# Windowed attention heads: two query blocks share one 512-column product per key tile

## The chip, the core and the metric

The kernel runs on one core of one Trainium2 chip. The metric is the device time of one execution in microseconds (us). Three runs of the kernel before gave 1479.55, 1479.58 and 1482.57 us; the median, 1479.58 us, is what a changed kernel is compared with.

## What is computed

The reference is a two-layer encoder trunk over 1024 tokens of width 1024. Only one part of its first layer matters here: eight "B" heads of width 64 in grouped-query attention (four query heads to one of two key heads), where a query sees the keys within 128 positions, plus a learned sink in the softmax:

```python
def window_gqa(q, k, v, sink, rel_bias):      # BLOCK = WINDOW = 128
    ...
    def one(args):                            # one block of 128 queries
        i, qblk = args
        kb = lax.dynamic_slice_in_dim(kp, i * BLOCK, 384, axis=1)
        vb = lax.dynamic_slice_in_dim(vp, i * BLOCK, 384, axis=1)
        s = jnp.einsum('bqkgd,bskd->bkgqs', qblk, kb) * scale + bias
        s = jnp.where(valid, s, -jnp.inf)
        m = jnp.maximum(jnp.max(s, axis=-1, keepdims=True), sk)
        p = jnp.exp(s - m)
        denom = jnp.sum(p, axis=-1, keepdims=True) + jnp.exp(sk - m)
        return jnp.einsum('bkgqs,bskd->bqkgd', p / denom, vb)
```

So each block of 128 queries meets its own tile of 128 keys and the tile on either side (two tiles in all at the two ends of the sequence).

## The kernel before, in words

All values are float32. A product is made from two rounded halves of each operand (a high part `h` and the remainder `l`, both in the format fp32r), so that one product becomes two or three matrix multiplications.

The program is built in Python; a planner then lays out the instructions of each engine from estimated times, priorities and dependencies. Program order sets the priority. `ahead(kind)` moves a step forward by a number of places (in this phase: scores 20, exponentials 60, splitting of a bank 150, closing 120; transposes and value products 0). `issue_after(x)` puts what follows behind instruction `x` on the same engine.

The phase "l0" works through layer 0: A heads and memory heads first, then the **band stage**, four calls of `window_pair` (L685) from `even`, each for two B heads (`i` = 0, 1 below, the "pair"). The stage lies about between 515 and 667 us of the span; the output projection of layer 0 (`out_project`, L1341 to L1376 in the profile) follows, and its first pieces are mixed into the last pair.

A call of `window_pair` goes over four groups `g` of two query blocks (`b` = 0, 1), that is blocks 2g and 2g+1:

- **Scores** (L710, L711): for each block and head, two multiplications into a bank `sa`; VectorE adds the bias, takes the running minimum and writes the tile `P` (L714). `P` holds both heads of one block; there are six such buffers, which later also receive the residual `xT` of the output projection (L1373).
- **Softmax**: ScalarE's exponentials (L725), VectorE's reciprocal (L727), then four **normalisations** on GpSimd (L732), in the order block 0 head 0, block 0 head 1, block 1 head 0, block 1 head 1.
- **Values**: `todo` lists the pairs (block, key tile), block 0 first: six pairs, or five in the first and last group. They are taken two at a time, in two or three steps `t`. In a step TensorE **transposes** four tiles of 128x128 of `P` (two pairs, two heads; L133) into one PSUM bank `tr` (two such banks); the transposes of steps 0 and 1 are written together ahead of step 0. ScalarE then copies the bank to `ph` (L125) and VectorE makes `pl` (L549). For each pair of the step two **value products** (L757) follow, one with the 256 columns of `ph` and one with those of `pl`, into the bank `pv` (one only). The columns of a pair go to two separate runs of 128 in that bank, since the bank is ordered head, block, query.
- **Closing**: the lower half of the bank is copied to `bt`, and L767 adds the halves into `y`.

Between these steps `pull(pulls)` inserts pieces of a projection that had been put off (L242: three multiplications of 512 columns each piece; two pieces at a time, one in the third pair). Such pieces stand behind the last score or transpose written before them. They are what TensorE does while the other engines prepare `P`, `ph` and `pl`.

Of the kernel before, what the change touches and what calls it, by code (L numbers as in the profile page):

```python
# [47 lines left out]
            c=(("P", "P"), ("P", "P"), ("P", "P"), ("yb", "yb"))),  # L48
       dict(y=(("P", "P", "q", "q", "v"), ("k", "k", "k", "k", "q", "q"), ("H",) * 6, ("H",) * 6, ("P", "P", "q", "q", "v"),
               ("k", "k", "k", "k", "q", "q"), ("H",) * 6),  # L50
            c=(("H", "H"), ("H", "H"), ("mk", "sg"), ("yb", "yb"))))
# [13 lines left out]
class Trunk:  # L65
# [619 lines left out]
    def window_pair(self, qs, ks, v, kv, h0, sink, y, pulls, side, lead=0):  # L685

        nc = self.nc
        kh, kl = ks
        bias = self.st("bias", [128, 2, 384])
        nc.sync.dma_start(bias, self.io["band"][h0:h0 + 2].rearrange("h p k -> p h k"))  # L690
        for g in range(4):
            st = self.tiny()
            nm, sm, r = (st[:, 4 * j:4 * j + 4] for j in range(3))
            pts = []
            o = self.ps("pv")
            ov = o.rearrange("p (h b q) -> p h b q", h=2, b=2)
            spans = []
            for b in range(2):
                blk = 2 * g + b
                lo, hi = max(0, blk - 1), min(8, blk + 2)  # L700
                n = (hi - lo) * 128
                bo = (lo - blk + 1) * 128
                spans.append((lo, hi, n))
                s = self.ps("sa", (128, 2, 512))
                pt = self.st("P", [128, 2, 385])
                nc.scalar.activation(pt[:, :, n:n + 1], sink[:, h0:h0 + 2][:, :, None], AF.Copy)
                for i in range(2):
                    q = qs[i][:, blk * 128:(blk + 1) * 128]
                    with self.ahead("score"):
                        nc.tensor.matmul(s[:, i, :n], q, kh[:, lo * 128:hi * 128], start=True, stop=False)  # L710
                        self.fence = nc.tensor.matmul(s[:, i, :n], q, kl[:, lo * 128:hi * 128], start=False, stop=True)  # L711
                    with self.ahead("exp"):
                        j = 2 * b + i
                        nc.vector.tensor_tensor_reduce(pt[:, i, :n], s[:, i, :n], bias[:, i, bo:bo + n], op0=OP.add,  # L714
                                                       op1=OP.min, scale=-1.0, scalar=sink[:, h0 + i:h0 + i + 1],
                                                       accum_out=nm[:, j:j + 1])
                pts.append(pt)
                if lead and g == 0:
                    self.pull(lead)
            with self.ahead("exp"):  # L720
                for b in range(2):
                    n = spans[b][2]
                    for i in range(2):
                        j = 2 * b + i
                        nc.scalar.activation(pts[b][:, i, :n + 1], pts[b][:, i, :n + 1], AF.Exp, bias=nm[:, j:j + 1],  # L725
                                             scale=-1.0, accum_out=sm[:, j:j + 1])
                nc.vector.reciprocal(r, sm)  # L727
                for b in range(2):
                    n = spans[b][2]
                    for i in range(2):  # L730
                        j = 2 * b + i
                        normal = nc.gpsimd.tensor_scalar(pts[b][:, i, :n], pts[b][:, i, :n], r[:, j:j + 1], 0.5,  # L732
                                                         op0=OP.mult, op1=OP.mult)
                self.normal = normal
            if g < 2:
                with self.tc.issue_after(normal.ins):
                    next(side, None)
            todo = [(b, c) for b in range(2) for c in range(spans[b][0], spans[b][1])]
            self.pull(pulls)
            made = {}  # L740
            for t in range(0, len(todo), 2):
                self.later_job(normal)
                two = todo[t:t + 2]
                for u in (t, t + 2):
                    if u not in made and u != 6 and u < len(todo) and t % 4 == 0:
                        tr = made[u] = self.ps("tr")
                        with self.ahead("flip"):
                            self.flip((tr[:, e * 256 + i * 128:e * 256 + (i + 1) * 128],
                                       pts[b][:, i, (c - spans[b][0]) * 128:(c - spans[b][0] + 1) * 128])
                                      for e, (b, c) in enumerate(todo[u:u + 2]) for i in range(2))  # L750
                parts = self.p_parts(made[t], 256 * len(two))
                self.pull(pulls)
                with self.ahead("pv"):
                    for e, (b, c) in enumerate(two):
                        for part in parts:
                            m = part[:, e * 256:(e + 1) * 256].rearrange("p (h q) -> p h q", h=2)
                            nc.tensor.matmul(ov[:, :, b, :], v[:, c, kv, :], m,  # L757
                                             start=(t + e == 0 and part is parts[0]),
                                             stop=(t + e == len(todo) - 1 and part is parts[1]), skip_group_check=True)
            bt = self.st("bt", [64, 512])  # L760
            with self.ahead("close"):
                self.copy(bt, o[64:128, :])
                for i in range(2):
                    p0 = 64 * i
                    dst = y[p0:p0 + 64].rearrange("p (b r c) -> p r b c", b=8, r=16)[:, 4 * g:4 * g + 4]
                    a, b = (x[0:64, i * 256:(i + 1) * 256].rearrange("p (r b c) -> p r b c", r=4, b=8) for x in (o, bt))
                    nc.vector.tensor_tensor(dst, a, b, op=OP.add)  # L767
# [1500 lines left out]
```

## Time and profile before

| what | value |
|---|---|
| median of three runs | 1479.58 us |
| profiled execution, whole | 1482.22 us |
| its span (first to last instruction) | 1480.4 us |
| TensorE busy | 1461.3 us (99%) |
| weight loads of TensorE busy (beside the multiplications) | 1254.1 us (85%) |
| VectorE, ScalarE, GpSimd busy | 1038.8, 839.2, 647.0 us |
| matrix multiplications, as many weight loads | 8049 |
| granted TensorE clock, mean | 0.998 |

PE is TensorE, PEld its weight loads, DVE VectorE, ACT ScalarE, POOL GpSimd, SP the engine that issues the transfers. The ends of matrix multiplications are modelled in the profile and they overlap their successors, so the time from the start of one to the start of the next says what one costs; the busy time of one is longer. In the rows of groups, the columns after the first bar are the group's busy time in us and the mean of one in ns; after the second bar stands the idle time of the engine just before them, and what ended it. In the timeline the columns are start, duration, engine, line, operation with its tiles, and how many alike were merged into the row; what stands in square brackets is idle time ahead of it.

### The profile page before, as it was taken

Reading aid. Unit: us, or ns where it says so; the run is one execution under the profiler, and the core shown is the slowest. Engines: PE = TensorE matmul, PEld = TensorE weight load, DVE = VectorE, ACT = ScalarE, POOL = GpSimd, SP = SyncE. Lnnn points to the kernel's source line nnn. Section 1 sums busy time; section 2 is a strip of 40 time slices with the busy share of each in tenths; the row PEclk is TensorE's granted clock in tenths of the full one; section 3 lists DMA queues with packets and bytes.
Section 4 is the critical chain, followed back from the end, with each engine's and each line's share of the span. In section 5 each row is a group of like instructions: output and inputs, shape, how many; then the busy total and the mean of one; then the engine's idle time right before and its main releaser. Section 6 shows DMA issues by size and latency. Waiting matters only on the chain.

```text
span 1480.4 us, 24751 instructions
## 1 busy us (share of the span) xinstructions
PE 1461.3 (99%) x8049; PEld 1254.1 (85%) x8049; DVE 1038.8 (70%) x2125; ACT 839.2 (57%) x1877; POOL 647.0 (44%) x766
## 2 busy tenths in 40 slices
PE   9999999999999999999999999999999999999997
PEld 8898888888888888888888887888888888888776
DVE  6687777777776678776687866654457787778584
ACT  7743665556655466655454544444456777776454
POOL 1223658566775656553450000002425556665355
PEclk9999999999999999999999999999999999999999
DMA  8966335334342524378553343567675568778844
GB/s 282 314 161 184 117 114 168 122 122 132 117 144 79 199 75 139 110 263 313 182 180 135 136 136 139 156 171 256 225 257 169 187 198 270 246 250 313 306 132 150
DMA packets 171809, 271.87 MB, mean 184 GB/s; under 512 B 15648, under 2 KB 92704, under 8 KB 170656
## 3 DMA queue, kind: packets, MB, share of 16 engines
q1 hardware_dynamic: 171248, 270.20, 56.6%
q8 instruction: 64, 1.05, 0.3%
q14 instruction: 65, 0.53, 0.1%
q10 hardware_dynamic: 432, 0.09, 0.0%
HBM read 174.28 MB, written 83.89 MB: 174 GB/s over the span
## 4 chain that ended last, share of the span: by engine, by line
PE 87%; DMA 4%; DVE 4%; ACT 2%; issue 1%; SPq 1%; POOL 0%; DVEq 0%; ACTq 0%; POOLq 0%
PE pj L242 16%; PE pj L62 12%; PE x L1650 7%; PE tr L133 6%; PE pv L1080 4%; PE y L1650 4%; PE pv L62 3%; PE s L62 3%; PE sa L1348 3%; PE tr L62 3%; PE pj L1348 2%; PE pv L1650 2%; PE sa L1046 2%; PE sa L1047 2%; PE s L1348 2%; PE tr L1348 2%
## 5 line engine op out<-in xcount | busy, mean ns | idle before, releaser
L549 DVE TENSOR_TENSOR pl<-tr,ph 128x512 fp32r<-128x512 f32 (+2 forms) x352 | 204.3, 594 | 45.2 <-ACT ph L125 43.3
L242 PE MATMUL pj<-H,wh 128*128 128x512 f32 x704 | 233.4, 412 | 0.4 <-DVE vt L313 0.2
L125 ACT ACTIVATE ph<-tr 128x512 fp32r<-128x512 f32 (+2 forms) x352 | 176.8, 523 | 99.6 <-PE tr L133 77.8
L158 POOL TENSOR_SCALAR wh<-wraw 128x512 fp32r<-128x512 f32 x48 | 30.4, 636 | 268.0 <-PE x L1650 233.2
L125 ACT ACTIVATE wh<-wraw 128x384 fp32r<-128x384 f32 (+1 forms) x163 | 89.2, 554 | 98.5 <-PE pj L1348 11.8
L242 PE MATMUL pj<-H,wl 128*128 128x512 f32 x352 | 139.0, 395 | 0.0
L242 PEld LDWEIGHTS pj<-H,wh 128*128 128x128 f32 x704 | 120.2, 189 | 18.2 <-issue 0.6
L62 PE MATMUL pj<-H,wh 128*128 128x512 f32 x384 | 121.0, 396 | 0.0
L1133 POOL TENSOR_SCALAR pn<-pn,st 128x384 f32<-128x384 f32 (+1 forms) x128 | 72.9, 572 | 99.3 <-DVE st L1132 57.5
L133 PE MATMUL tr<-ident,P 128*128 128x128 f32 x752 | 115.3, 273 | 0.8 <-DVE pl L549 0.5
L1295 POOL TENSOR_TENSOR wl<-wraw,wh 128x384 fp32r<-128x384 f32 x56 | 63.5, 1135 | 89.7 <-ACT wh L125 78.7
L1131 ACT ACTIVATE pn<-pn,st 128x384 f32<-128x384 f32 (+1 forms) x128 | 75.1, 587 | 40.4 <-DVE st L1128 38.9
L133 PEld LDWEIGHTS tr<-ident,P 128*128 128x128 f32 x752 | 88.8, 140 | 9.5 <-DVE pl L549 1.8
L1052 ACT ACTIVATE P<-sa,st 128x1024 f32<-128x1024 f32 x64 | 71.5, 1117 | 34.4 <-DVE st L1051 16.9
L1054 POOL TENSOR_SCALAR P<-P,st 128x1024 f32<-128x1024 f32 x64 | 73.8, 1155 | 27.5 <-DVE st L1053 27.2
L1051 DVE TENSOR_REDUCE st<-sa 128x1 f32<-128x1024 f32 x64 | 77.5, 1218 | 8.0 <-PE sa L1047 7.4
L62 PE MATMUL s<-k,q 128*128 128x384 f32 (+1 forms) x352 | 81.4, 327 | 0.7 <-DMA k<-k 0.7
L242 PEld LDWEIGHTS pj<-H,wl 128*128 128x128 f32 x352 | 66.2, 188 | 15.2
L62 PE MATMUL pj<-H,wl 128*128 128x512 f32 x192 | 75.6, 394 | 0.0
L160 POOL TENSOR_TENSOR wl<-wraw,wh 128x512 fp32r<-128x512 f32 x52 | 71.3, 1373 | 9.6 <-ACT wh L125 7.2
L62 PEld LDWEIGHTS pj<-H,wh 128*128 128x128 f32 x384 | 66.6, 188 | 5.4
L864 PE MATMUL pj<-ah,H 128*128 128x256 f32 x384 | 70.7, 282 | 0.3 <-ACT ah L125 0.2
(574 smaller groups left out, 4170.0 us busy)
## 6 DMA issues: line engine op xcount, KB each, us to landing
y<-yb SPq DMA_DIRECT2D x24, 512.0 KB, 3.9
wraw<-s SPq DMA_DIRECT2D x64, 192.0 KB, 3.8
wraw<-w_e SPq DMA_DIRECT2D x44, 256.0 KB, 3.5
k<-k SPq DMA_DIRECT2D x42, 256.0 KB, 5.5
s<-bias SPq DMA_DIRECT2D x56, 192.0 KB, 2.0
wq<-w_o SPq DMA_DIRECT2D x40, 256.0 KB, 3.3
y<-sg SPq DMA_DIRECT2D x18, 512.0 KB, 3.5
wraw<-w_o SPq DMA_DIRECT2D x36, 256.0 KB, 4.3
```

Of the source, the lines that this page charges most:

```text
L62: return lambda *a, **k: self.tc.keep_in_program_order(getattr(self.engine, name)(*a, **k))
L125: return self.nc.scalar.activation(out, in_, AF.Copy, scale=scale)
L133: self.turned = self.fence = self.pe.transpose(o, i, self.ident)
L242: self.pe.matmul(a[:, :n], s[:, kt % UNIT, :], m, start=(kt == 0 and i == 0), stop=(kt == KT - 1 and i == 2))
L549: self.low = nc.vector.tensor_tensor(pl[:, :n], tr[:, :n], ph[:, :n], op=OP.subtract)
L1051: nc.vector.tensor_reduce(st[:, 0:1], s, axis=AX.X, op=OP.max, negate=True)
L1052: nc.scalar.activation(pt, s, AF.Exp, bias=st[:, 0:1], accum_out=st[:, 1:2])
L1054: self.normal = nc.gpsimd.tensor_scalar(pt, pt, st[:, 2:3], 0.5, op0=OP.mult, op1=OP.mult)
L1131: nc.scalar.activation(o, o, AF.Exp, bias=st[:, 0:1], scale=-1.0, accum_out=st[:, 2:3])
L1133: self.normal = normal = nc.gpsimd.tensor_scalar(o, o, st[:, 3:4], 0.5, op0=OP.mult, op1=OP.mult)
L1348: last = nc.tensor.matmul(bank, s[:, k, :], y[3 * u + k][m][:, cols], start=start and u + k + e == 0, stop=u == 1 and k + e == 4, skip_gro ...
L1650: self.last = nc.tensor.matmul(bank, ws[s][:, k, :], b[k][m], start=start and k + i == 0, stop=k == UNIT - 1 and i == 2, skip_group_check= ...
```

## The change

The order of the value products is regrouped. The two blocks of a group always share exactly two key tiles (2g and 2g+1). Steps 0 and 1 now take one shared tile each, for both blocks: the four transposes of a step are block 0 head 0, block 0 head 1, block 1 head 0, block 1 head 1 of that key tile, placed in the bank in the order head, block, query. Their value products are two multiplications of 512 columns in one run, instead of four of 256 columns. Step 2 takes the tiles that only one block meets (two pairs, or one in the first and last group) as before, with 256 columns. The number of transposes, splits and pulled pieces, and the places at which they stand in the program, stay as they were; which tiles each of them works on changes.

```diff
-            todo = [(b, c) for b in range(2) for c in range(spans[b][0], spans[b][1])]
+            both = range(spans[1][0], spans[0][1])
+            todo = [[(b, c) for b in range(2)] for c in both]
+            todo.append([(b, c) for b in range(2) for c in range(spans[b][0], spans[b][1]) if c not in both])
             self.pull(pulls)
             made = {}
-            for t in range(0, len(todo), 2):
+            for t, two in enumerate(todo):
                 self.later_job(normal)
-                two = todo[t:t + 2]
-                for u in (t, t + 2):
-                    if u not in made and u != 6 and u < len(todo) and t % 4 == 0:
-                        tr = made[u] = self.ps("tr")
-                        with self.ahead("flip"):
-                            self.flip((tr[:, e * 256 + i * 128:e * 256 + (i + 1) * 128],
-                                       pts[b][:, i, (c - spans[b][0]) * 128:(c - spans[b][0] + 1) * 128])
-                                      for e, (b, c) in enumerate(todo[u:u + 2]) for i in range(2))
+                at = lambda e, b, i: i * 256 + b * 128 if t < 2 else e * 256 + i * 128
+                for u in ((0, 1), (), (2,))[t]:
+                    tr = made[u] = self.ps("tr")
+                    with self.ahead("flip"):
+                        self.flip((tr[:, at(e, b, i):at(e, b, i) + 128],
+                                   pts[b][:, i, (c - spans[b][0]) * 128:(c - spans[b][0] + 1) * 128])
+                                  for e, (b, c) in enumerate(todo[u]) for i in range(2))
                 parts = self.p_parts(made[t], 256 * len(two))
                 self.pull(pulls)
                 with self.ahead("pv"):
+                    if t < 2:
+                        for part in parts:
+                            nc.tensor.matmul(o, v[:, two[0][1], kv, :], part, start=t == 0 and part is parts[0], stop=False,
+                                             skip_group_check=True)
+                        continue
                     for e, (b, c) in enumerate(two):
                         for part in parts:
                             m = part[:, e * 256:(e + 1) * 256].rearrange("p (h q) -> p h q", h=2)
-                            nc.tensor.matmul(ov[:, :, b, :], v[:, c, kv, :], m,
-                                             start=(t + e == 0 and part is parts[0]),
-                                             stop=(t + e == len(todo) - 1 and part is parts[1]), skip_group_check=True)
+                            nc.tensor.matmul(ov[:, :, b, :], v[:, c, kv, :], m, start=False,
+                                             stop=e == len(two) - 1 and part is parts[1], skip_group_check=True)
```

## The prediction

> **What bounds the kernel now.** I first read the chain of work that ended last on the profile's page, to see whether any engine but TensorE decides.
>
> ```profile
> PE 87%; DMA 4%; DVE 4%; ACT 2%; issue 1%; SPq 1%; POOL 0%; DVEq 0%; ACTq 0%; POOLq 0%
> ```
>
> Then the busy times in three stretches: before the band stage, most of the band stage, and the rest (the columns are stretch, its length, then busy time and count for each engine, the granted clock, the share of the transfer engines and GB/s).
>
> ```profile
> 0.00:515.00 515.00, 508.80 (x3180) 449.70 (x3181) 371.36 (x674) 301.26 (x632) 271.84 (x318) 1.00 0.53 162
> 515.00:654.00 139.00, 137.19 (x781) 118.74 (x781) 105.14 (x242) 86.37 (x227) 80.62 (x107) 1.00 0.40 133
> 654.00:1480.40 826.40, 815.32 (x4090) 685.68 (x4088) 562.27 (x1210) 451.53 (x1018) 294.56 (x343) 1.00 0.63 206
> ```
>
> TensorE carries the chain, and in the band stage it is idle for only 139.00 - 137.19 = 1.81 us at a clock of 1.00. VectorE is at 105 of 139 us. So the change is worth what it takes out of TensorE's queue, plus or minus what it does to 1.81 us of waiting. For the first term I need the price of a multiplication, from the groups by line and shape:
>
> ```profile
> L242 PE MATMUL pj<-H,wl 128*128 128x512 f32 x352 | 139.0, 395 | 0.0
> ...
> L757 PE MATMUL pv<-ph,v 128*128 128x256 f32 x88 | 23.3, 284 | 0.6 <-DVE yb L767 0.6
> ...
> L757 PEld LDWEIGHTS pv<-ph,v 128*128 128x128 f32 x88 | 16.6, 189 | 1.9 <-ACT ph L125 1.0
> ```
>
> By these means, four products of 256 columns (4 x 284 ns) would cost far more than two of 512 (2 x 395). But the modelled ends overlap the next start. The timeline of TensorE in the first pair shows what one really takes, from start to start:
>
> ```profile
> 521.06 0.62 PE L242 MATMUL pj<-H,wh 128*128 128x512 f32 x2
> ...
> 524.55 0.34 PE L710 MATMUL sa<-k,q 128*128 128x384 f32 x1
> ...
> 526.98 0.28 PE L757 MATMUL pv<-ph,v 128*128 128x256 f32 x1
> ...
> 527.93 0.34 PE L710 MATMUL sa<-k,q 128*128 128x384 f32 x1
> ```
>
> Between 521.06 and 524.55 stand 15 multiplications of 512 columns and nothing else: 3.49 / 15 = 0.233 us each. Between 526.98 and 527.93 stand eight value products: 0.95 / 8 = 0.119 us each. The columns are what costs; two of 256 take 0.238, one of 512 takes 0.233.
>
> **The change part by part.** *Fewer, wider products.* There are 16 groups (four pairs of four). In each, steps 0 and 1 held eight products of 256 columns and now hold four of 512: 8 x 0.119 - 4 x 0.233 = 0.02 us a group, 0.3 us over 16. The 64 multiplications and 64 weight loads that go are off the queue with that; the loads run beside the products and their 64 x 189 ns count for nothing, as long as the row holds that eight products with eight loads come every 0.119 us. Term: -0.3 us.
>
> The Trainium skill, "TensorE: Matmul & The Clock Gate", section "Back-to-back issue gap", gives two prices: columns/2.4 + 2.5 ns for a single product, and for a stream of loads and products about 81 ns at 128 columns and about 131 at 512. By the first, 64 fewer products are worth 64 x 2.5 ns = 0.16 us, an estimate close to the row. By the second, a straight line gives 98 ns at 256 columns, an estimate of 32 x (4 x 98 - 2 x 131) ns = 4.2 us, a gain that could be measured. The trace has 233 ns where that rule has 131, so the trace decides against the second and the sum does without it.
>
> *The wait for the remainder.* In steps 0 and 1 the first product (of `ph`) now covers 0.233 us ahead of the first that needs `pl`, where it covered 0.119. The waits of TensorE in the band stage:
>
> ```profile
> PE pv L757 <- DVE pl L549: 0.8, 2, 0.5
> ```
>
> Two waits for `pl`, both in step 0 of a group of the third pair; each shrinks by 0.114 us at most, since VectorE makes `pl` no sooner. Term: between 0 and -0.2 us, and I take -0.2. A gain above that is excluded, because splits, closings and their engines are untouched.
>
> *The transposes of step 0 need the second block.* Until now the first four transposes needed only block 0 (in the first group of a pair, both banks: block 0, then block 1). Now the third and fourth need block 1's two normalisations, which GpSimd does last. Behind them on TensorE's queue are the other bank's transposes, the pulled pieces tied to them and the value products, and ScalarE's copy to `ph` waits for them. Where it costs nothing, the transposes already start after all four normalisations, as in the second group of the first pair:
>
> ```profile
> 514.67 2.29 POOL L732 TENSOR_SCALAR P<-P,st 128x384 f32<-128x384 f32 x4 [2.83 <-DVE st L727]
> ```
>
> ```profile
> 518.55 0.60 PE L133 MATMUL tr<-ident,P 128*128 128x128 f32 x4
> ```
>
> They are done at 516.96 and the transposes start at 518.55. Going through the 16 groups in this way, I find the third and fourth transposes ready in 14. Two are not: the first groups of the third and fourth pair.
>
> ```profile
> 583.88 2.62 POOL L732 TENSOR_SCALAR P<-P,st 128x256 f32<-128x256 f32 x4
> ```
>
> ```profile
> 585.72 0.49 PE L133 MATMUL tr<-ident,P 128*128 128x128 f32 x3
> ...
> 586.40 0.71 PE L133 MATMUL tr<-ident,P 128*128 128x128 f32 x4
> ```
>
> ```profile
> 621.96 2.37 POOL L732 TENSOR_SCALAR P<-P,st 128x256 f32<-128x256 f32 x4 [9.69 <-DVE st L727]
> ```
>
> ```profile
> 623.22 0.92 PE L133 MATMUL tr<-ident,P 128*128 128x128 f32 x4
> ...
> 624.38 0.55 PE L133 MATMUL tr<-ident,P 128*128 128x128 f32 x3
> ```
>
> In the third pair the last normalisation ends at 583.88 + 2.62 = 586.50, while the fourth transpose of the first bank (the last of the three at 585.72) started at about 585.94: it would start 0.56 us later. In the fourth pair the end is 624.33, and the fourth (the third of the four at 623.22) started at about 623.44: 0.89 us later. If nothing fills the gap, that is 1.5 us. But the second bank had to wait for the same last normalisation already: its transposes ended near 586.84 + 0.27 and 624.65 + 0.27, and with four transposes from 586.50 and 624.33 on (0.11 us apart) they would end some 0.1 us after that; the scores that stand between the two banks can be issued in the gap. Only if the planner leaves them behind is the whole 1.5 us lost. Term: +0.2 to +1.5, and I take +0.3, since the same scores fill these places today.
>
> *Buffers.* Block 0's last tile is now transposed in step 2 in the groups that have a tile of block 0 alone (all but the first), where it was in step 1: its `P` buffer comes free one step later, three to five us. Inside the band stage a buffer is wanted again three groups later, with slack. In the last pair it is the residual loads of the output projection that want it, on SP's queue:
>
> ```profile
> 634.08 0.82 SPq L1373 DMA_DIRECT2D P<-xT  x2
> ...
> 658.17 0.90 SPq L1373 DMA_DIRECT2D P<-xT  x2
> 659.11 0.43 SPq L1373 DMA_DIRECT2D yb<-xT  x1
> 660.88 0.33 SPq L1341 DMA_DIRECT2D wraw<-s  x1
> ```
>
> ```profile
> 637.18 0.60 PE L133 MATMUL tr<-ident,P 128*128 128x128 f32 x4
> ...
> 657.14 0.60 PE L133 MATMUL tr<-ident,P 128*128 128x128 f32 x4
> ...
> 661.30 0.38 PE L133 MATMUL tr<-ident,P 128*128 128x128 f32 x2
> ```
>
> The first pair of loads can then go no earlier than about 637.4 instead of 634.08, and the pair at 658.17 (behind the transposes at 657.14) no earlier than about 661.6 (behind those at 661.30). The planner knows this and can put other loads ahead; if it doesn't, the weight load at 660.88 goes after 661.6 + 0.90 + 0.43 = 662.9, 2.0 us late. Term: 0 to +2.0 for the queue; I take 0, since that load's weights are fetched ahead and TensorE shows no wait for transfers there.
>
> The sum: -0.3 - 0.2 + 0.3 + 0 = -0.2 us. The profiled execution took 1482.22 us whole (1.8 us around its span), which is 2.6 us above the median of the runs, so the profile of the changed kernel would be near 1482.0 like for like, and the median 1479.58 - 0.2 = 1479.4. A measurement of this kernel can tell about 0.2%, 3.0 us, from no change; the three runs alone lie that far apart. By the bounds of the terms, this case reaches from 1479.1 to 1482.6 (+1.5, +2.0, -0.5 all at once), and 1478.0 to 1481.5 is its likely part.
>
> **The rivals.** *Weight loads bind.* A load is busy for 189 ns, longer than the 119 ns spacing of 256 columns. If a load cost what it is longer, each of the 64 that go would give 70 ns: 4.5 us, 1475.1. The Trainium skill's price for a stream, above, comes out at nearly the same. For it: loads are busy 118.74 of 139 us in the stage. Against it: eight products with eight loads at 0.119 us. I give it 0.06.
>
> *A lucky order.* The order of every engine is planned from estimated times, and from the first group on these differ; the change may clear waits that it isn't aimed at. If all 1.81 us of the band stage went, with the 0.5 us above and as much again of the 11.08 us that TensorE is idle after 654, the time is 1479.58 - 4.1 = 1475.5. For it: the waits are few and long, so one change of order can remove one. Against it: no part of the change shortens what they wait for. 0.10.
>
> *The later buffers hold up the transfers of the output projection* (the slow side). Besides the 2.0 us on SP's queue at 660.88, the two loads at 634.08 (128 x 512 x 4 bytes each, 0.52 MB) move out of a quiet stretch into a full one (the same columns as above):
>
> ```profile
> 630.00:640.00 10.00, 10.00 (x58) 8.78 (x57) 7.57 (x20) 5.87 (x16) 4.32 (x7) 1.00 0.41 145
> 640.00:650.00 10.00, 10.00 (x59) 8.61 (x58) 7.77 (x16) 7.66 (x18) 6.70 (x8) 1.00 0.98 339
> ```
>
> At 339 GB/s they take 1.5 us there, and everything behind them comes that much later. Together 3.5 us, 1479.58 - 0.2 + 3.5 = 1482.9. It decides as soon as what is fetched ahead for the output projection covers less than the delay: one weight tile feeds nine products of 512 columns, 9 x 0.233 = 2.1 us, and there are four buffers. For it: from 640 on the transfer engines are full. Against it: TensorE is busy for all of both stretches, so there is some cover. With other unlucky orders I give this side 0.24.
>
> **How the numbers follow.** Forecast 0.60, weight loads 0.06, lucky order 0.10, late transfers 0.24. Faster by over 0.2% are the second and third together, 0.16; within 0.2% the forecast, 0.60; slower 0.24. The range reaches from the lucky order, 1475.5, to just above the late transfers, 1483.2; outside it lie the weight loads and the tails of the two orders.
>
> **What would show it.** Right: L757 with 64 products of 512 columns and 48 of 256, four of the former 0.93 us from start to start; waits of L757 for `pl` of 0.5 to 0.8 us; the first bank of the first groups of pairs three and four ending with the last normalisation; TensorE idle in the band stage between 1.3 and 3.3 us. Wrong: products of 512 columns closer together than 0.22 us, the residual loads at L1373 with weight loads queued behind them and TensorE waiting at L1348, or a new order with several us more or less idle time after 654 us.

## The result, and the profile after

The changed kernel took 1484.76 us (median of 22 runs, 1481.91 to 1488.79), the kernel before, run beside it, 1481.66 us (22 runs, 1479.2 to 1484.7). The ratio is 1.0022, interval 1.0014 to 1.0030: slower by 2.1 to 4.4 us, where the forecast had 0.2 us faster. Two later comparisons of the same two kernels gave 1.0027 (1.0017 to 1.0038) and 1.0013 (1.0003 to 1.0023). The three runs that the prediction started from are the first of these 22, and their median, 1479.58 us, lies 2 us below that of all 22, so ratios are what is compared below. The profiled execution of the changed kernel took 1481.91 us, the fastest of its 22 runs, so its total says little; its stages are read one by one.

In the band stage the profile shows what was forecast. First the groups of the value products (L757 is now the wide product, L763 the narrow one):

```profile
L757 PE MATMUL pv<-pl,v 128*128 128x512 f32 x32 | 13.1, 410 | 0.6 <-DVE pl L549 0.6
L757 PE MATMUL pv<-ph,v 128*128 128x512 f32 x32 | 12.8, 400 | 0.3 <-DVE yb L772 0.3
...
L763 PE MATMUL pv<-ph,v 128*128 128x256 f32 x24 | 7.2, 306 | 0.0
L763 PE MATMUL pv<-pl,v 128*128 128x256 f32 x24 | 7.0, 307 | 0.0
```

Then four wide products in the timeline of TensorE, in the first pair:

```profile
525.56 0.39 PE L757 MATMUL pv<-ph,v 128*128 128x512 f32 x1
525.79 0.40 PE L757 MATMUL pv<-pl,v 128*128 128x512 f32 x1
526.02 0.39 PE L757 MATMUL pv<-ph,v 128*128 128x512 f32 x1
526.25 0.39 PE L757 MATMUL pv<-pl,v 128*128 128x512 f32 x1
```

There are 64 of 512 columns and 48 of 256, and the four start 0.23 us apart. The waits of TensorE in the band stage (us in total, times, longest):

```profile
PE pv L757 <- DVE pl L549: 0.6, 2, 0.5
PE tr L133 <- POOL P L732: 0.4, 2, 0.2
PE pv L757 <- DVE yb L772: 0.3, 1, 0.3
```

Before they were 0.8, 0.2 and 0.6 us. The last of the three, a wait for the closing, is 0.3 us shorter without having been forecast. In the first group of the last pair, which the prediction had singled out, GpSimd's normalisations end at 620.42 + 2.35 = 622.77, and the last transposes of the bank follow at once:

```profile
620.42 2.35 POOL L732 TENSOR_SCALAR P<-P,st 128x256 f32<-128x256 f32 x4 [9.68 <-DVE st L727]
```

```profile
622.46 0.42 PE L710 MATMUL sa<-k,q 128*128 128x384 f32 x1
...
622.89 0.38 PE L133 MATMUL tr<-ident,P 128*128 128x128 f32 x2
```

A score (622.46) fills the gap between the first and the last transposes, as was assumed. If each multiplication of the changed kernel is paired with its counterpart in the kernel before, the stretch from 515 to 640 us is 0.73 us shorter (from start to start).

The loss lies behind the band stage. The same three stretches in both kernels (columns: stretch, length, busy time and count of PE, PEld, DVE, ACT and POOL, granted clock, transfer share, GB/s); before:

```profile
640.00:720.00 80.00, 80.00 (x371) 65.40 (x370) 54.56 (x84) 42.12 (x84) 35.69 (x32) 1.00 0.79 276
720.00:800.00 80.00, 79.61 (x361) 64.69 (x360) 61.05 (x105) 40.94 (x76) 28.90 (x23) 1.00 0.58 186
...
1228.00:1262.00 34.00, 33.56 (x203) 30.02 (x202) 26.70 (x84) 24.64 (x64) 21.84 (x30) 1.00 0.77 258
```

and after:

```profile
640.00:720.00 80.00, 78.61 (x356) 63.55 (x355) 54.41 (x83) 41.29 (x82) 32.87 (x30) 1.00 0.80 278
720.00:800.00 80.00, 79.60 (x360) 64.65 (x359) 61.60 (x107) 40.92 (x76) 29.00 (x23) 1.00 0.58 186
...
1228.00:1262.00 34.00, 32.55 (x193) 28.40 (x193) 26.70 (x86) 24.85 (x66) 21.73 (x30) 1.00 0.76 243
```

TensorE's idle time is length minus busy time. From 640 to 720 us it goes from 0 to 1.39, from 1228 to 1262 from 0.44 to 1.45, and 720 to 800 is unchanged in this execution. The clock is 1.00 in all of them.

**640 to 720 us, the output projection.** SP's queue after:

```profile
637.30 2.48 SPq L1378 DMA_DIRECT2D P<-xT  x4
639.88 0.38 SPq L1256 DMA_DIRECT2D H<-y  x1
...
646.35 0.95 SPq L1256 DMA_DIRECT2D H<-y  x2
...
684.19 0.94 SPq L1256 DMA_DIRECT2D v<-y  x2
685.23 0.38 SPq L1256 DMA_DIRECT2D H<-y  x1
```

Before, two of these four residual loads `P<-xT` stood at 634.08, and two here:

```profile
639.56 0.87 SPq L1373 DMA_DIRECT2D P<-xT  x2
...
641.00 1.49 SPq L1251 DMA_DIRECT2D H<-y  x3
```

Now all four stand in one block just ahead of the operand loads `H<-y`. The first two `H<-y` behind the block take 7.1 and 7.2 us to land (5.4 and 5.6 before), and the next two are issued at 646.35, behind loads of weights, `k` and `q`, where before they were issued at 642.02 and 643.93. Further on, two `v<-y` loads stand at 684.19 ahead of a row of `H<-y` loads; before, they came behind that row, at 691.37. ScalarE, which splits the operands, waits for the loads (in brackets: idle time ahead, and what ended it):

```profile
646.99 0.63 ACT L125 ACTIVATE H<-H 128x512 fp32r<-128x512 f32 x1 [1.92 <-DMA H<-y]
...
690.31 0.63 ACT L125 ACTIVATE H<-H 128x512 fp32r<-128x512 f32 x1 [2.54 <-DMA H<-y]
```

Behind these splits, in order, stand the ones that make the weights' halves, so the remainders `wl` come late and TensorE waits for them:

```profile
652.33 0.51 PE L1353 MATMUL sa<-q,wl 128*128 128x512 f32 x1 [0.66 <-DVE wl L1300]
...
701.66 0.50 PE L1353 MATMUL pj<-H,wl 128*128 128x512 f32 x1 [0.73 <-DVE wl L1300]
```

From start to start these two waits cost 0.82 and 0.89 us. The planner also puts some 40 of TensorE's own products between 640 and 720 us at other places than before, but no other step from one product to the next takes over 0.15 us longer than is usual for its width, so the loss lies in the two waits.

**1228 to 1262 us, in layer 1.** Here no engine's order differs between the two kernels. What lands later is the store `y<-yb` issued at 1215.99 before and at 1215.54 after. Before (the column behind KB is the time from issue to landing):

```profile
y<-yb SPq DMA_DIRECT2D x1, 512.0 KB, 8.3
```

and after, over the time of its flight, with the fetch queue that has a packet in it:

```profile
q8 instruction: 1, 0.02, 0.6%
...
y<-yb SPq DMA_DIRECT2D x1, 512.0 KB, 9.8
```

VectorE needs the buffer of that store. Before:

```profile
1224.35 0.68 DVE L1172 TENSOR_TENSOR yb<-pv,bt 64x512 f32<-64x512 f32 x1
```

After:

```profile
1225.45 0.68 DVE L1177 TENSOR_TENSOR yb<-pv,bt 64x512 f32<-64x512 f32 x1 [1.48 <-DMA y<-yb]
```

Everything behind it on VectorE comes later, and between 1228 and 1262 us TensorE waits for `pl` where the kernel before has 0.4 us:

```profile
PE tr L62 <- DVE pl L549: 1.3, 2, 0.8
```

The queue q8 is TensorE's own instructions: by the packet records it moves one packet of 16,384 bytes, a fetch, for every 256 instructions of TensorE (64 packets for 16,388 recorded instructions before, 63 for 16,251 after), mostly in about 1 us (0.88 to 1.70 us in the profile before). The change takes 128 multiplications and loads and nine semaphore waits out of TensorE's queue, and from the band stage on every fetch falls 137 instructions later in the work. So a fetch lies in the flight of this store that wasn't there before. The store isn't alone: `bm<-offsets`, issued 1 us ahead of it, takes 9.8 us instead of 7.9, while `v<-v`, which lands before the fetch starts, takes 6.8 instead of 6.7.

### The profile page after: what moved, and what is told of

The parts are those of the page before. It is cut to its first block, busy times and chain, and to the rows that moved or that the text cites. A ratio compares the mean times of both kernels' runs of the same rounds, so it can differ in the third digit from the quotient of the medians.

```text
span 1480.1 us, 24606 instructions
## 1 busy us (share of the span) xinstructions
PE 1459.5 (99%) x7985; PEld 1250.5 (84%) x7985; DVE 1038.8 (70%) x2125; ACT 838.4 (57%) x1877; POOL 646.4 (44%) x766
## 3 DMA queue, kind: packets, MB, share of 16 engines
q8 instruction: 63, 1.03, 0.3%
## 4 chain that ended last, share of the span: by engine, by line
PE 86%; DMA 5%; DVE 4%; ACT 2%; issue 2%; SPq 1%; POOL 0%; DVEq 0%; ACTq 0%; POOLq 0%
PE pj L242 16%; PE pj L62 12%; PE x L1655 7%; PE tr L133 6%; PE pv L1085 4%; PE y L1655 4%; PE pv L62 3%; PE s L62 3%; PE pj L1353 3%; PE tr L62 3%; PE sa L1353 3%; PE pv L1655 2%; PE s L1353 2%; PE sa L1051 2%; PE sa L1052 2%; PE tr L1353 2%
```

## The experiments

The first four runs had two theories. A: the loss comes from the last pair, through the transfers of the output projection. B: it lies in the band stage itself.

**The first three pairs only** (the last pair as before):

```
+            if h0 < 6:
+                both = range(spans[1][0], spans[0][1])
+                todo = [[(b, c) for b in range(2)] for c in both]
...
+            else:
+                todo = [(b, c) for b in range(2) for c in range(spans[b][0], spans[b][1])]
...
```

> The change in the first three pairs of heads only; the last pair, whose buffers the residual loads of the output projection take over, is as before, and the order of all transfers is that of before. Theory A (the loss of 3.1 us comes from the transfers of the output projection, which are ordered and released differently only through the last pair): no loss, 0.0 to -0.6 us against before, ratio 0.9996 to 1.0000, and no wait of TensorE in the output projection. Theory B (the loss is in the band stage itself: transposes and splits that wait for the second block, or a 512-column product that costs more than it seems): three quarters of it, +2.3 us, ratio about 1.0016.

Measured: 1.0020 (1.0010 to 1.0031), some 3 us slower. A alone is wrong: SP's order is as before here, and TensorE is never idle between 640 and 720 us.

```profile
640.00:720.00 80.00, 80.00 (x370) 65.45 (x369) 55.38 (x85) 42.28 (x86) 36.43 (x32) 1.00 0.81 279
720.00:800.00 80.00, 78.12 (x353) 63.19 (x352) 61.48 (x103) 38.73 (x73) 30.52 (x24) 1.00 0.59 184
```

But 720 to 800 us has 1.88 us of idle time. There a fetch, at 729.3 us, took 2.38 us by the packet records, and three loads in flight at the time, two `wraw<-w_oe` and `x<-P`, took 5.7 to 5.9 us, where before they took 4.2 to 4.5.

**The last pair only** (`h0 == 6` in the same place):

> The change in the last pair only. Theory A: the whole loss, +3 us, ratio about 1.002, with waits of TensorE for weights or operands between 645 and 710 us. Theory B: a quarter, +0.8 us, ratio about 1.0005.

Measured: 1.0026 (1.0015 to 1.0037). B is wrong: three pairs as before, and the whole loss is there, with 1.79 us of idle time from 640 to 720.

**The new order with narrow products** (the transposes, banks and order of the changed kernel, but four products of 256 columns for a shared tile):

```
-                        for part in parts:
-                            nc.tensor.matmul(o, v[:, two[0][1], kv, :], part, start=t == 0 and part is parts[0], stop=False,
-                                             skip_group_check=True)
+                        for e in range(2):
+                            for part in parts:
+                                nc.tensor.matmul(o[:, e * 256:(e + 1) * 256], v[:, two[0][1], kv, :], part[:, e * 256:(e + 1) * 256],
+                                                 start=t + e == 0 and part is parts[0], stop=False, skip_group_check=True)
```

> The changed order of tiles and bank layout everywhere, but every product of a shared tile is again two of 256 columns, so only the width goes back. Theory A: as slow as the changed kernel, +3.1 us and 0.3 to 0.5 more, ratio about 1.0023. If the width were the cause: as before, ratio 1.0000.

**The changed kernel again**, beside these:

> The changed kernel once more, beside the three others on the same chip and for a second profile. Both theories: ratio about 1.002, +3 us. Theory A says that this profile, too, loses in the output projection (645 to 710 us), by more than the 1.8 us of the first profile if it is a typical run, and gains 0.4 to 0.6 us between 515 and 645.

Measured: 1.0015 (1.0005 to 1.0024) for the narrow products, 1.0027 for the changed kernel. With narrow products TensorE's queue is only nine instructions shorter than before; 640 to 720 us has 1.91 us of idle time, the other two stretches hardly more than before. So the loss in the output projection needs no wide product. The rest (the two intervals overlap) looked like something that goes with the number of instructions. Neither A nor B explained both the first and the second run; theory C, the shifted fetches, was added here.

**The first three pairs, with TensorE's queue at its old length.** Behind every wide product two empty instructions are issued, and seven more at the end:

```
+                                wide = nc.tensor.matmul(o, v[:, two[0][1], kv, :], part, start=t == 0 and part is parts[0], stop=False,
+                                                        skip_group_check=True)
+                                with self.tc.issue_after(wide.ins):
+                                    for _ in range(2 + 7 * (h0 == 4 and g == 3 and t == 1 and part is parts[1])):
+                                        nc.tensor.nop("pad")
```

> The first three pairs changed, the last one as before, and 103 empty instructions of TensorE put back behind the wide products (two behind each of 48, seven more at the end of the third pair): TensorE's queue is then again as long ahead of everything behind the band stage as in the kernel before. Theory C (TensorE fetches its queue 256 instructions, 16,384 bytes, at a time; each fetch holds up the transfers in flight by one to two us; a queue that is 103 instructions shorter moves every later fetch to another place of the work): the 3.0 us that the first three pairs cost go, ratio to the kernel before 0.9995 to 1.0005; the fetches between 640 and 800 us of the span within 2 us of those of the kernel before (660, 688, 718, 745, 777), and no wait of TensorE at 750 to 770. Without C (the loss is in the band stage or in the orders that its change brings): still about 1.0020.

Measured: 0.9997 (0.9984 to 1.0010), where the same kernel without them had 1.0020. The fetches are at 661, 689, 718, 744 and 776 us, and the three stretches have 0, 0.42 and 0.46 us of idle time.

**The kernel before with 153 empty instructions in front:**

```
+        for _ in range(153 if h0 == 0 else 0):
+            nc.tensor.nop("pad")
```

They wait for nothing, so the planner puts them early in TensorE's queue: 95 in the first 20 us, and 58 between 140 and 149 us (with 119 of them, further on, 24 stand there). Three products between 49 and 61 us also change places.

> The kernel before with nothing changed but 153 empty instructions of TensorE among the first ones of its queue, long ahead of the band stage, so that every later fetch of instructions stands where it stands with the first three pairs changed (153 more is the same as 103 fewer, by 256). No product, no transfer and no order of any other engine changes. Theory C: slower by 1.5 to 3 us (1.0010 to 1.0020), with the loss in stretches behind the band stage where a fetch meets a row of operand loads (fetches at about 651, 674, 699, 729, 757, a wait of TensorE at 750 to 770); in the stretches ahead of the band stage it can fall either way. Without C: 1.0000, and at most 153 x 0.01 us more.

Measured: 1.0041 (1.0029 to 1.0053). The direction is C's, the size is above its range. Behind the band stage the stretches have 0, 1.86 and 1.43 us of idle time, the fetch at 730.3 us takes 2.40 us, and a wait of 1.46 us follows at 752. But the shift applies ahead of the band stage too, and by 500 us this execution was 1.95 us behind the one before.

**The whole change with the residual loads moved**: the four loads `P<-xT`, and the additions that use them, are written behind the second of the operand loads on SP's queue.

```
...
+        behind = self.y_loads[1]
+        for i in range(0, 0 if last else 4):
+            with self.tc.issue_after(behind.ins):
+                residual(at(c11, i), i, 1)
...
```

> The whole change, but the four first residual loads of the output projection stand on SP's queue behind the first operand loads of that stage instead of ahead of them. Theory A (that block of loads, moved from a quiet stretch to just ahead of the operand loads, makes the operands late): the two waits of TensorE at 651 and 700 us go or shrink to under 0.5 us in all, the stretch from 640 to 720 us is within 0.5 us of that of the kernel before instead of 1.8 to 2.3 above it, and the ratio to the kernel before falls from 1.0022 to 1.0027 to about 1.0010. If A is wrong: the two waits stay, 1.0025.

**The same with 137 empty instructions:**

> The whole change, with the loads as in the run beside it and with 137 empty instructions of TensorE put back as well (two behind each wide product, nine more at the end of the last pair). If A and C hold and are all there is: the gain that was forecast for the band stage is left, -0.2 to -0.6 us, ratio 0.9995 to 1.0003. A alone: as the run beside it. C alone: about 1.0013 (the 2 us of the output projection left). Neither: 1.0025.

Measured: 1.0016 (1.0006 to 1.0026) and 1.0015 (1.0004 to 1.0027). Theory A as put here was half right. The wait at 651 us is gone in both (the first has one of 0.5 us at 669 instead), the one at about 701 us is not (1.04 and 1.03 us more than the pace of the products): the planner still puts the two `v<-y` loads ahead of the `H<-y` loads. The 137 empty instructions make no difference to the time here. The block of residual loads is only the first of the moves that the later buffers bring about. The theory became A': the later release of `P` changes the whole order that the planner lays out for these transfers.

**The kernel before with the residual loads later** tests that with the program of the products untouched:

```
-            with self.tc.issue_after(self.fetched.ins) if last else nullcontext():
+            with self.tc.issue_after(self.fetched.ins if last else self.sent.ins):
                 nc.sync.dma_start(x, res[nt][:, 512 * (2 - half):512 * (3 - half)])
```

> The kernel before, with every value product as it was; only the residual loads of the output projection of layer 0 are put behind the spill of y (L498) on SP's queue, which is about where the changed kernel has them, since it frees their buffers one step later. Theory A' (the later buffers change the order of the transfers that the planner lays out: the residual loads ahead of the operand loads at 640 us, and as a knock-on two v loads ahead of six H loads at 684 us): the two waits of TensorE at about 651 and 700 us appear, 640 to 720 us takes 1.5 to 2.4 us longer, ratio 1.0010 to 1.0017. Were the loss due to the products or transposes of the last pair themselves: 1.0000.

Measured: 1.0016 (1.0007 to 1.0026). From this one delay the planner makes nearly the order of the changed kernel, the `v<-y` loads included. SP's queue in this kernel:

```profile
638.32 1.84 SPq L1373 DMA_DIRECT2D P<-xT  x4
...
641.00 0.41 SPq L1251 DMA_DIRECT2D H<-y  x1
```

and TensorE has both waits:

```profile
654.07 0.50 PE L1348 MATMUL sa<-q,wl 128*128 128x512 f32 x1 [1.51 <-DVE wl L1295]
...
703.13 0.50 PE L1348 MATMUL pj<-H,wl 128*128 128x512 f32 x1 [0.56 <-DVE wl L1295]
```

with 2.07 us of idle time in the stretch from 640 to 720 us. From start to start the two waits cost 1.67 and 0.73 us, which is the 2.4 us of the ratio; some 40 of TensorE's products there change places in this kernel too, and no other step there takes over 0.15 us longer than is usual.

**The kernel before with 119 empty instructions in front** (119 more is 137 fewer, by 256):

> The kernel before with 119 empty instructions of TensorE among its first ones, nothing else: later fetches of instructions stand as in the changed kernel (119 more is the same as 137 fewer, by 256; about 647, 671, 702, 733, 758 us). Theory C: slower by what is left of the loss of the changed kernel when A' is taken off, 1 to 2 us (1.0005 to 1.0015), by waits of TensorE behind a fetch of over 2 us; 640 to 720 us as in the kernel before. Without C: 1.0000.

Measured: 1.0022 (1.0013 to 1.0030), above the range expected. 640 to 720 us is as before, and the store in layer 1 meets its fetch; in the time of its flight:

```profile
q8 instruction: 1, 0.02, 0.6%
...
y<-yb SPq DMA_DIRECT2D x1, 512.0 KB, 9.4
```

```profile
1224.80 0.68 DVE L1174 TENSOR_TENSOR yb<-pv,bt 64x512 f32<-64x512 f32 x1 [1.10 <-DMA y<-yb]
```

Between 1228 and 1262 us it has 1.30 us of idle time, 0.9 more than the kernel before. The other 2 us or so of this run's loss were not located.

**Both at once:**

> Both of the runs beside it at once: the loads behind the spill and 119 empty instructions. If A' and C are the whole loss, this kernel, in which no product, transpose or split is changed, is as slow as the changed kernel: 1.0022 to 1.0030, and more than either of the two alone. If the two are not what costs: 1.0000 to 1.0010.

Measured: 1.0037 (1.0024 to 1.0051). With no product, transpose or split changed this is at least as slow as the changed kernel, and about as slow as its two parts together (1.0016 and 1.0022); it is above the range expected, as the run with 119 alone was.

**64 empty instructions in front:**

> The kernel before with 64 empty instructions in front: every fetch a quarter of its period earlier (about 653, 681, 710, 738, 769 us). Theory C: the time depends on the place alone, so this differs from the kernel before by -1 to +3 us; a loss only with a fetch of over 1.8 us in the records that TensorE's waits follow. Were the empty instructions themselves what costs in the earlier run with 153 of them (+6.1 us), 64 would cost about 64/153 of it, 2.6 us, in the stretch where they stand, and nothing behind it.

Measured: 1.0012 (1.0003 to 1.0021). Here all three stretches are as in the kernel before (0, 0.44 and 0.52 us), and no fetch lies in the flight of the store (8.4 us). So its loss of about 1.8 us shows in none of these stretches, and it was not located. By 500 us this profile is 1.50 us behind that of the kernel before and the one with 153 is 1.95 us behind, but the two with 119 are 0.49 and 0.63 us ahead, and the 12 profiles whose instructions are the same as before up to there lie between 1.76 us ahead and 1.02 us behind. That empty instructions in front cost something by themselves is thus neither shown nor excluded; the changed kernel has none. For what lies behind the band stage it is unlikely, since there 64 of them go with no loss and 153 with up to 2.5 us of idle time.

**The changed kernel with 137 empty instructions, the changed kernel once more, and the last pair alone with 34:**

> The whole change with 137 empty instructions of TensorE put back and the loads as the planner lays them. Theory C as well as A': the fetches are where the kernel before has them (660, 688, 718, 745, 777 us, each within 3), the two waits at 651 and 700 us stay, and the ratio is that of A' alone, 1.0012 to 1.0017, some 0.0008 below the changed kernel beside it. A' alone in this kernel: the same as the changed kernel, 1.0022 to 1.0027.

> The changed kernel beside the padded one: 1.0022 to 1.0027 by every theory, as in its two earlier comparisons.

> The last pair alone changed, 34 empty instructions put back. A' and C: 1.0012 to 1.0017, where the last pair without them had 1.0026. A' alone: 1.0026 again.

Measured: 1.0014 (1.0002 to 1.0026), 1.0013 (1.0003 to 1.0023) and 1.0017 (1.0009 to 1.0026). The padded kernels are where A' alone has them, but the changed kernel beside them came out as fast as the padded one, as it was with the loads moved (1.0016 and 1.0015). By the times alone the share of the fetches in the changed kernel is therefore not shown. One expectation failed in the profile as well: in the padded changed kernel the wait at about 651 us, which was to stay, is gone. The profiles, each of a single execution, do separate the two causes. This table has length minus busy time of TensorE in the three stretches, and the time of the store in layer 1 from issue to landing; three values are three profiles.

| kernel | TensorE's queue behind the band stage, instructions | ratio | idle 640-720 | idle 720-800 | idle 1228-1262 | store, us |
|---|---|---|---|---|---|---|
| before | 0 | 1 | 0.00 | 0.39 | 0.44 | 8.3 |
| three pairs, padded | 0 | 0.9997 | 0.00 | 0.42 | 0.46 | 8.3 |
| 64 in front | +64 | 1.0012 | 0.00 | 0.44 | 0.52 | 8.4 |
| residual loads late | 0 | 1.0016 | 2.07 | 0.44 | 0.48 | 8.3 |
| narrow products | -9 | 1.0015 | 1.91 | 0.39 | 0.56 | 8.4 |
| last pair only | -34 | 1.0026 | 1.79 | 0.67 | 0.62 | 8.5 |
| last pair, padded | 0 | 1.0017 | 1.04 | 0.67 | 0.39 | 8.2 |
| changed, padded | 0 | 1.0014 | 0.53 | 0.67 | 0.44 | 8.3 |
| changed, loads moved, padded | 0 | 1.0015 | 0.96 | 0.40 | 0.49 | 8.3 |
| changed, loads moved | -137 | 1.0016 | 1.23 | 0.54 | 1.29 | 9.4 |
| changed | -137 | 1.0022, 1.0027, 1.0013 | 1.39, 1.23, 1.67 | 0.40, 2.36, 1.33 | 1.45, 1.48, 1.42 | 9.8, 10.1, 9.9 |
| 119 in front | +119 | 1.0022 | 0.00 | 0.39 | 1.30 | 9.4 |
| 119 and residual loads late | +119 | 1.0037 | 1.72 | 1.37 | 0.99 | 9.0 |
| three pairs | -103 | 1.0020 | 0.00 | 1.88 | 1.08 | 9.1 |
| 153 in front | +153 | 1.0041 | 0.00 | 1.86 | 1.43 | 9.8 |

The first column of idle time is exactly 0 in the six kernels that have the residual loads early and 0.53 to 2.07 us in the others. How large it is there varies even with nearly the same order of the loads (0.53 in the changed kernel with empty instructions, 1.23 to 1.67 without), and why isn't shown. The column from 1228 to 1262 us follows the place of the fetches: in the eight profiles of the last six rows a packet of q8 lies in the flight of the store, it takes 9.0 to 10.1 us, and TensorE is idle for 0.99 to 1.48 us; in the other nine no packet does, the store takes 8.2 to 8.5 us, and the idle time is 0.39 to 0.62. The column from 720 to 800 us follows it less well: it is worst (1.86 to 2.36) where the fetch at 729 to 735 us took 2.2 to 2.4 us, in three profiles, but with the fetches of the changed kernel it is anything from 0.39 to 2.36.

Idle time understates the loss. By paired multiplications, from start to start, 640 to 720 us takes 1.9, 1.9 and 2.4 us longer in the three profiles of the changed kernel and 2.5 us longer with the residual loads late, and 0.0 in the five other kernels that have them early. From 1228 to 1262 us it is 0.7 to 1.8 us longer in the eight profiles with a fetch in the flight, and at most 0.2 in the rest.

## Why the prediction was wrong

*Fewer, wider products, the wait for the remainder, the transposes* (-0.3, -0.2, +0.3): the sum has the right sign and about half the size. By paired multiplications the stretch from 515 to 640 us is shorter by 0.42 us on average over the six profiles that hold the whole change (three of them the changed kernel itself, three with its loads or its queue mended; from 0.17 to 0.73 shorter), and by 0.03 us over the five with the band stage as before (from 0.07 shorter to 0.01 longer). The forecast of the three terms was -0.2. That it came so close is in part luck: the kernel with the new order and narrow products gains 0.45 us in the same stretch, so its one profile gives the width no share, and the shorter wait for the closing was in no term. The four wide products 0.23 us apart also decide against the second price of the Trainium skill, "TensorE: Matmul & The Clock Gate", section "Back-to-back issue gap", which gives a stream about 131 ns at 512 columns.

*Buffers* is the step that failed: "Term: 0 to +2.0 for the queue; I take 0, since that load's weights are fetched ahead and TensorE shows no wait for transfers there." The prediction looked at a weight load at 660.88 behind the last residual loads. Its rows of SP's queue left out the residual loads at 639.56 and 647.14, which stand right beside the operand loads. What is late are those operand loads `H<-y`, and through ScalarE's and VectorE's order the remainders `wl`; TensorE waits at L1353, which was L1348 before, as the prediction had put down for being wrong. That TensorE showed no wait there was the state of an order that the change replaced. The run that delays only the residual loads prices it: 1.0016, 2.4 us (1.0 to 3.9). The rival of the late transfers had named the residual loads, the full stretch and 3.5 us, and got 0.24. Its price was of the right kind; its account, transfer time and cover of weight tiles, missed that the planner lays out some 24 transfers of SP's queue at other places as a consequence.

*The 64 loads and multiplications that go* counted only for their time in the queue. That a queue shorter by 137 instructions moves all later fetches of instructions was in no step and no rival. Between 1228 and 1262 us the changed kernel has 1.0 us more idle time in each of its three profiles (1.45, 1.48 and 1.42 against 0.44), between 720 and 800 us 0, 2.0 and 0.9. By paired multiplications the band stage and the three stretches behind it come together to 2.7, 5.7 and 4.5 us in these profiles, and the three comparisons to 3.3, 4.0 and 1.9; a profile is a single execution, so the two agree in size only. In time, putting the empty instructions back took away the loss of the first three pairs (1.0020 to 0.9997) and perhaps a part of that of the last pair (1.0026 to 1.0017, with intervals that overlap), but none of that of the whole change (1.0013 to 1.0014).

The time itself, 1484.76, lies above the range's end of 1483.2; of that, some 2 us come from the start, since the median of three that it was added to, 1479.58, lies that far below the 1481.66 of all 22 runs. The forecast's own number, the difference, was off by 3.5 us.

What stays open: where the kernels with empty instructions in front lose the part that no stretch here shows; how much of the changed kernel's time the fetches cost beside the transfers; and why one fetch takes 0.9 us and another, at nearly the same place, over 2.2. No version here was faster than the kernel before: the three pairs with the old queue length come to 0.9997 with an interval on both sides of 1, so the gain is there in the band stage and too small to measure in the whole.

## What to carry to other kernels

A buffer that is freed one step later is a change to whoever takes it next, and where a planner orders the transfers, to everything that it lays out after it: look for the next taker in the profile, compare the order of the queue that feeds it, and price the operands that then land late. When the stages that a change touches come out as forecast and the total doesn't, put back the number of instructions with empty ones before looking for a cause in the code: a difference of some 0.2% can be nothing but the shifted fetches.

## What the runs showed of the hardware

TensorE's instructions come over the transfer engines beside the data, by the packet records of q8: 16,384 bytes for 256 instructions, as one packet of 0.88 to 2.40 us. A store of 512 KB that is in flight at the time lands 0.5 to 1.9 us later (9.0 to 10.1 us against 8.2 to 8.5, in 17 profiles). The Trainium skill, "Runtime: NRT & Kernel Launch", section "Instruction fetch mechanics", has the blocks of 16 KiB and 256 instructions, which the count of 64 packets bears out, and calls the cost of crossing one mostly hidden. For most of the 64 that agrees with the traces: in the profile before, TensorE loses under 0.3 us in the 10 us behind 56 of them. For the ones that meet a transfer with an engine waiting behind it, it doesn't: 1.0 us more idle time of TensorE at one such place.
